# Rebuilding an expert router's chain, and gathering tokens by pairs of experts from one fp32 copy

## The chip, the core and the metric

The kernel runs on one core of one Trainium2 chip. The metric is the device time of one run in microseconds (us). The kernel before was run three times: median 1444.87 us, 1441.94 to 1446.6.

## What is computed

Two blocks of a network are applied to 256 tokens of width D = 1024. The first block is a mixer (a gMLP and an RWKV-7 recurrence side by side) and a hierarchical mixture of experts; the second is two layers of attention and feed-forward. Each sublayer's input is normalised, then scaled and shifted by vectors that are themselves products of a conditioning vector c with a weight matrix (the modulation). The change lies in the end of the mixer and in the mixture of experts:

```python
x = x + gate1[:, None, :] * y
h = _modulate(_rmsnorm(x, norm2_g[l]), shift2, scale2)
...
group_prob = jax.nn.softmax((ht @ rg_w + rg_b).astype(f32), axis=-1)
g_p, g_idx = lax.top_k(group_prob, 1)
exp_logits = (ht @ re_w + re_b).astype(f32).reshape(N, N_GROUPS, EXPERTS_PER_GROUP)
sel = jnp.take_along_axis(exp_logits, g_idx[:, :, None], axis=1)[:, 0]
e_p, e_idx = lax.top_k(jax.nn.softmax(sel, axis=-1), TOP_K)
e_p = e_p / jnp.sum(e_p, axis=-1, keepdims=True)
weights = g_p * e_p
...
return (jax.nn.silu(xbk @ w_gate[e]) * (xbk @ w_up[e])) @ w_down[e]
```

So a token picks one of 4 groups, then two of that group's 8 experts; the two results are added with their weights. There are 32 experts with a hidden width of 512; the three weight matrices of each are 2.1 MB in fp32, and all of them are read.

## The kernel before, in words

Everything is fp32, and the 256 tokens lie on the partitions in two halves i of 128. TensorE (PE) multiplies, VectorE (DVE), ScalarE (ACT) and GpSimd (POOL) do the rest, SyncE (SP) issues the loads.

**Modulation** (L179 to L241) is a generator. One step loads 256 rows of a weight matrix (1.05 MB) and multiplies them with c in 16 small matmuls into a PSUM buffer; DVE adds it to a sum in SBUF. Four steps make one of the vectors. Steps are spread over the kernel: `fill(n)` takes the next n, `need(j)` takes as many as vector j wants (L246 to L253), and tables (FILL_A, L33, and others) say how many are taken at which place. Eight are taken at the end of the recurrence, in front of the output projection (FILL_A[3]).

**The end of the mixer.** `project_out(kt)` (L845 to L867) turns one of eight slices of the mixer's output, splits it and the weights in high and low fp32r halves, and adds three products to four PSUM buffers, two halves of the tokens by two halves of the columns. L928 to L942 run it for all eight and add the gated result to x, one buffer of 128x512 after the other.

**The router** (L946 to L1049). x is turned (L963 to L967), multiplied with the 36 columns of router weights (L971), and scaled by the inverse norm (L973, L978). Then comes a chain of small DVE instructions: the maximum of the groups, the selected group's 8 logits, first and second maximum among them (`first_max`, L984 to L995), a mask M of 32 experts and the weights Wt (L1026 to L1032), the number of the largest count (L1039 to L1045) and the position of each token within its expert (L1047). The scale and shift of the modulation are brought to the layout of the gathered tokens (GS, L1052 to L1071). The normalised x is then written in two fp32r halves, xh by ACT and xl by a subtraction on POOL (L1074 to L1081), with the width in another order, because a weight row block takes every eighth column.

**Loads of expert weights** (L1084 to L1107). Each load is 1.05 MB, half a matrix. They go to 14 rotating slots (4 + 6 + 2 + MORE, where MORE is 2, L27). 18 loads are issued ahead of the first expert, in the order ORDER (L31); four of them go to buffers that have another use later (EARLY, L30), the twelfth to one of the two buffers of gathered tokens.

**The experts.** 64 slots are reserved for each expert; a pair j of experts fills 128 partitions. `gather(quad)` (L1187 to L1205) makes for two pairs a one-hot matrix D4 from the positions and, for each of eight slices of the width, four fp32r matmuls of 128x256 (two halves of tokens, high and low) into a PSUM buffer of their own; DVE and ACT in turn evict them with scale and shift to xg. `widen(j)` (L1207, matmuls L1216) multiplies with 4 loads of gate weights, and again with 4 of up weights; `gated` and `turned` (L1222, L1230) make the activation and turn it; `places(j)` (L1234 to L1249) turns the one-hot matrix back; `narrow(j)` (L1251, matmuls L1261) multiplies with 4 loads of down weights; `scatter(j)` (L1274, matmuls L1280 and L1282) adds the weighted result to the tokens. The loop (L1292 to L1320) takes pairs 0 to 9 and then 10 to 15. PE's order in it is the written one (`manual_schedule`): gate of pair j, turning of j-1, scatter of j-2, places of j-1, up of j, the gather for the next two pairs where j is odd, down of j-1. The other engines' order is a list scheduler's. After pair 9 a branch (`crowded`, L1119) looks whether any expert has more than 64 tokens; with these inputs none has, and the branch is not taken.

**Two lines elsewhere.** Behind the experts, `flip` (L358 to L412) turns and evicts a PSUM buffer twice, by ACT (L367) and by DVE (L379), which both read the same buffer.

## Time and profile before

| | |
|---|---|
| median of three runs | 1444.87 us (1441.94 to 1446.6) |
| the profiled execution | 1445.49 us |
| its span in the profile | 1443.7 us |
| PE busy (weight loads beside it: 1002.3 us) | 1356.1 us, 94% |
| DVE busy | 763.9 us, 53% |
| ACT busy | 576.5 us, 40% |
| POOL busy | 77.9 us |
| DMA | 400.42 MB, 277 GB/s in the mean |
| PE's granted clock, mean | 0.977 of full speed |

The profile is of one execution; times within it count from the start of its span. A busy engine is one with an instruction in work; a share over the whole span is a mean of stages with different limits, so the table alone doesn't tell what bounds a stage. The granted clock is 0.5 (1.2 GHz) or 1.0 (2.4 GHz) at a moment, and a mean over a stretch.

### The profile page before, as it was taken

To read this page: it belongs to the slowest core of one execution; us is meant where nothing else is said; L and a number is where in the kernel's file an instruction comes from. 1 tells how busy PE (TensorE), PEld (TensorE's weight loads), DVE (VectorE), ACT (ScalarE), POOL (GpSimd) and SP (SyncE) were. 2 spreads that over 40 slices of the span, in tenths; PEclk is the share of its full clock that TensorE was granted. 3 is DMA by queue.
4 is the path that set the end of the run, shared out by engine and by line. 5 is a ranking of instruction groups with operands and counts; after the bars stand their busy time and mean duration, and the time that the engine had idled before them with its cause. 6 is when DMAs were issued, how large, how long until landed. Compare 5 with 4: busy or idle time off the path is not lost.

```text
span 1443.7 us, 22926 instructions
## 1 busy us (share of the span) xinstructions
PE 1356.1 (94%) x9330; PEld 1002.3 (69%) x9330; DVE 763.9 (53%) x1507; ACT 576.5 (40%) x1020; POOL 77.9 (5%) x79
## 2 busy tenths in 40 slices
PE   6999999699999988989979989999998999999997
PEld 5888878444444434534348867899996897799997
DVE  5648767511221111111165885888876575766565
ACT  3543013411111111101166755554456685654544
POOL 1002000100000000000020230000021001100000
PEclk9989999799999999999989999999999999999999
DMA  9826479599999999999967564988775534555540
GB/s 361 295 69 251 164 274 380 226 365 426 426 427 426 427 427 402 391 426 427 427 246 252 196 228 146 336 276 311 286 248 181 172 117 149 184 196 196 178 150 30
DMA packets 138688, 400.42 MB, mean 277 GB/s; under 512 B 6562, under 2 KB 84658, under 8 KB 114003
## 3 DMA queue, kind: packets, MB, share of 16 engines
q1 hardware_dynamic: 138578, 398.91, 72.0%
q8 instruction: 75, 1.23, 0.3%
q14 instruction: 35, 0.28, 0.1%
HBM read 397.82 MB, written 1.05 MB: 276 GB/s over the span
## 4 chain that ended last, share of the span: by engine, by line
PE 44%; DMA 9%; DVE 3%; ACT 3%; issue 1%; POOL 0%; POOLq 0%; DVEq 0%; SPq 0%; ACTq 0%
PE pmm L416 8%; PE pmm L417 8%; PE pmm L418 8%; PE pacc L416 5%; PE pacc L417 5%; PE pacc L418 5%; DMA wruns<-in_moe_w_gate_dram 4%; DMA wruns<-in_moe_w_down_dram 3%; DMA wruns<-in_moe_w_up_dram 2%; PE pmm L190 1%; PE pmm L1261 1%; ACT sqj L294 1%; PE pmm L366 1%; PE pmm L1622 1%; PE pmm L435 1%
## 5 line engine op out<-in xcount | busy, mean ns | idle before, releaser
L416 PE MATMUL pmm<-hh,whi 128*128 128x256 f32 (+1 forms) x1040 | 296.4, 285 | 2.0 <-ACT whi L167 2.0
L418 PE MATMUL pmm<-hh,wlo 128*128 128x256 f32 (+1 forms) x1040 | 297.1, 286 | 0.2 <-DVE wlo L168 0.2
L417 PE MATMUL pmm<-hl,whi 128*128 128x256 f32 (+1 forms) x1040 | 295.5, 284 | 0.0
L1216 PE MATMUL pmm<-wruns,xg 128*64 128x512 f32 x1024 | 233.1, 595 | 7.1 <-DMA wruns<-in_moe_w_gate_dram 7.1
L168 DVE TENSOR_TENSOR wlo<-wcols,whi 128x1024 fp32r<-128x1024 f32 (+1 forms) x130 | 168.4, 1300 | 99.3 <-ACT whi L167 98.8
L416 PEld LDWEIGHTS pmm<-hh,whi 128*128 128x128 f32 (+1 forms) x1040 | 197.6, 190 | 8.6 <-issue 3.6
L417 PEld LDWEIGHTS pmm<-hl,whi 128*128 128x128 f32 (+1 forms) x1040 | 196.6, 189 | 1.4
L418 PEld LDWEIGHTS pmm<-hh,wlo 128*128 128x128 f32 (+1 forms) x1040 | 197.0, 189 | 0.6 <-DVE wlo L168 0.4
L167 ACT ACTIVATE whi<-wcols 128x1024 fp32r<-128x1024 f32 (+1 forms) x130 | 136.1, 1053 | 119.0 <-PE pmm L417 91.7
L1216 PEld LDWEIGHTS pmm<-wruns,xg 128*64 128x64 f32 x1024 | 81.8, 137 | 141.1 <-issue 115.8
L168 DVE TENSOR_TENSOR wlo<-wrows,whi 128x1024 fp32r<-128x1024 f32 x87 | 108.1, 1248 | 56.3 <-ACT whi L167 55.9
L167 ACT ACTIVATE whi<-wrows 128x1024 fp32r<-128x1024 f32 x87 | 91.7, 1061 | 90.5 <-PE pmm L417 45.5
L1261 PE MATMUL pmm<-wruns,em 128*64 128x512 f32 x512 | 118.4, 595 | 7.2 <-DMA wruns<-in_moe_w_down_dram 5.7
L1261 PEld LDWEIGHTS pmm<-wruns,em 128*64 128x64 f32 x512 | 38.5, 137 | 79.3 <-issue 62.4
L1270 ACT ACTIVATE o<-ay 128x512 fp32r<-128x512 f32 x32 | 20.2, 631 | 177.5 <-DVE ay L1269 177.5
L1269 DVE SCALAR_TENSOR_TENSOR ay<-pmm,wsl,ga 128x512 f32<-128x512 f32 x32 | 24.0, 751 | 105.8 <-PE pmm L1261 103.8
L1307 DVE TENSOR_TENSOR ay<-ay,pmm 128x512 f32<-128x512 f32 x16 | 11.0, 688 | 120.0 <-PE pmm L1216 120.0
L1248 DVE COPY wsl<-pmm 64x1 f32<-64x1 f32 x32 | 5.0, 156 | 130.7 <-PE pmm L1245 130.4
L417 PE MATMUL pacc<-wlo,ah 128*128 128x512 f32 x176 | 69.2, 393 | 0.0
L416 PE MATMUL pacc<-whi,ah 128*128 128x512 f32 x176 | 68.9, 391 | 0.0
L418 PE MATMUL pacc<-whi,al 128*128 128x512 f32 x176 | 68.6, 393 | 0.0
L1222 ACT ACTIVATE ay<-pmm 128x512 f32<-128x512 f32 x16 | 9.6, 598 | 109.4 <-PE pmm L1216 109.4
(533 smaller groups left out, 2217.3 us busy)
## 6 DMA issues: line engine op xcount, KB each, us to landing
wruns<-in_moe_w_gate_dram SPq DMA_DIRECT2D x64, 1024.0 KB, 19.5
wruns<-in_moe_w_up_dram SPq DMA_DIRECT2D x64, 1024.0 KB, 19.5
wruns<-in_moe_w_down_dram SPq DMA_DIRECT2D x64, 1024.0 KB, 19.6
wrows<-in_w_mod_dram SPq DMA_DIRECT2D x48, 1024.0 KB, 7.0
wcols<-in_w_ffn_gate_dram SPq DMA_DIRECT2D x22, 1024.0 KB, 5.2
wcols<-in_w_ffn_up_dram SPq DMA_DIRECT2D x22, 1024.0 KB, 6.3
wrows<-in_w_ffn_down_dram SPq DMA_DIRECT2D x22, 1024.0 KB, 5.2
wrows<-in_ada_w_dram SPq DMA_DIRECT2D x16, 1024.0 KB, 7.7
```

Source lines behind the costliest of these rows:

```text
L167: ACT.activation(hi, src, AF.Copy)
L168: (POOL if ahead else DVE).tensor_tensor(lo, src, hi.bitcast(F32), op=OP.subtract)
L190: PE.matmul(p[32 * g:32 * g + 32, 0:n].rearrange("p (a j) -> p a j", j=32), lhsT, groups(rhs)[:, g], start=first, stop=last, skip_group_ch ...
L294: ACT.activation(j, src, AF.Square, accum_out=ss)
L366: PE.matmul(p, src[:, i, 128 * kt:128 * kt + 128], dg[i], start=True, stop=True)
L416: PE.matmul(p, a[0], b[0], start=first, stop=False, skip_group_check=True)
L417: PE.matmul(p, a[0], b[1], start=False, stop=False, skip_group_check=True)
L418: PE.matmul(p, a[1], b[0], start=False, stop=last, skip_group_check=True)
L1216: PE.matmul(p[64 * a:64 * a + 64, :], xg[:, kt, lc(2 * j + a)], wt[a][:, k, :], start=kt == 0, stop=kt == KT - 1, skip_group_check=True)
L1261: PE.matmul(pd[n][64 * a:64 * a + 64, :], hT[:, f, 64 * a:64 * a + 64], wt[a][:, b, 512 * n:512 * n + 512], start=f == 0, stop=f == 3, ski ...
L1269: DVE.scalar_tensor_tensor(yf, pd[n], wsl, ga2[:, ns], op0=OP.mult, op1=OP.mult)
L1270: ACT.activation(oh[:, ns], yf, AF.Copy)
```

## The change

It edits five things.

- **The end of the mixer.** `project_out` is split: turning and splitting stay in it, the products move to `project_on(kt, i, w)`. The last two slices are done for tokens 0 to 127 first, then for tokens 128 to 255, and the gated sum of the first half runs while the second half's products do. The preparation of the router's weights (G2, rw, rb) is moved ahead of slice 4. The sums of squares of x are started per half.
- **The router.** PE, DVE and ACT get a written order. The transposes go by token half and four slices into one PSUM buffer. Maxima are taken over all 8 rows (two token halves by four groups) of 8 experts at once, and the chosen group is applied to the mask at the end. The mask and the counting matmuls are fp32r. The weights Wt are computed after the first one-hot matrix; the largest count (`most_`) moves into the loop, behind the gather of pair 1. Temporaries lie in one buffer `scr`.
- **Modulation.** Three of the eight steps in front of the output projection (FILL_A[3] 8 to 5) are taken behind the logits, and `need(5, 6, 7)` stands behind the issue of the weight loads. From there on `hold` is set and is not reset: the products of steps 1 to 3 of a vector are added up in one PSUM buffer, step 3 ends with an extra `yield`, and DVE adds the buffer in the step after it.
- **The gather.** xh and xl give way to one fp32 copy xr, written by ACT alone; POOL's subtraction goes. `gather(j)` works for one pair: eight slices of two fp32 matmuls of 128x128, four slices to a PSUM buffer, each slice evicted behind its own matmuls by DVE and ACT in turn. The gathered tokens go to a half of `xx`, which before that holds the transposed x. In the loop the gather of pair j+1 follows the up matmuls of pair j, for every j within a group.
- **Loads.** MORE is 4 instead of 2 (16 rotating slots), three buffers instead of four are used early, and 19 loads are issued ahead.

The function `crowded` is adapted to the new names. The core of the diff:

```diff
 BIG = 6
-MORE = 2
+MORE = 4
 GROUPS = (range(0, 10), range(10, 16))
 
-EARLY = {4: "em", 3: "ay", 11: "oo", 12: "xg"}
-ORDER = (0, 1, 2, 5, 6, 7, 8, 9, 10, 3, 4, 11, 12, 13, 14, 15, 16, 17)
-
-FILL_A = (0, 0, 2, 8, 0, 2)
+EARLY = {4: "em", 3: "ay", 11: "oo"}
+ORDER = (0, 1, 2, 5, 6, 7, 8, 9, 10, 3, 4, 11, 12, 13, 14, 15, 16, 17, 18)
+
+FILL_A = (0, 0, 2, 5, 0, 2)
 FILL_P = (0, 4, 2)
 FILL_E = 3
...
+    hold = []
...
-                    p = gv[-1]()
+                    held = bool(hold) and q > 0
+                    if not held or q == 1:
+                        p = gv[-1]()
                     for kt in range(2 * q, 2 * q + 2):
-                        products(p, cb(kt), wt[:, kt % 2, :], kt == 2 * q, kt == 2 * q + 1)
-                    if q == 0:
+                        products(p, cb(kt), wt[:, kt % 2, :], kt == (2 if held else 2 * q), kt == (7 if held else 2 * q + 1))
+                    if held and q == 3:
+                        yield
+                    if held and q < 3:
+                        pass
+                    elif q == 0:
                         ACT.activation(acc, p[:, 0:256], AF.Copy)
                     else:
                         DVE.tensor_tensor(acc, p[:, 0:256], acc, op=OP.add)
@@ -859,12 +866,14 @@
                 DVE.tensor_tensor(yl[:, kt, :], yf, yh[:, kt, :].bitcast(F32), op=OP.subtract)
             if kt % 2 == 0:
                 w_out.append(load_rows(A["w_out"][0], 128 * kt))
...
+            return split_w(w_out[-1][:, kt % 2:kt % 2 + 1, :])
+
+        def project_on(kt, i, hl):
+            hi, lo = hl
+            ts = slice(128 * i, 128 * i + 128)
+            for n in range(2):
+                ns = slice(512 * n, 512 * n + 512)
+                mm3(op[i][n], (yh[:, kt, ts], yl[:, kt, ts]), (hi[:, 0, ns], lo[:, 0, ns]), kt == 0, kt == 7)
...
+
+        G2, S2 = G1, modc[:, 3, :]
         DVE.scalar_tensor_tensor(G2, modc[:, 4, :], 1.0, colr("n2g", 8), op0=OP.add, op1=OP.mult)
...
+        for kt in range(4, 6):
+            w = project_out(kt)
             for i in range(2):
...
+                project_on(kt, i, w)
+
+        w = [project_out(kt) for kt in (6, 7)]
         for i in range(2):
...
+            for kt in (6, 7):
+                project_on(kt, i, w[kt - 6])
+        rr = [Rstd() for _ in range(2)]
+        halves = [slice(0, 512), slice(512, 1024)]
+        with tc.manual_schedule(engines=MAN):
+            for i in range(2):
+                for n, ns in enumerate(halves):
+                    xs = x_sb[:, i, ns]
+                    DVE.tensor_tensor(op[i][n], op[i][n], ga[:, n, :], op=OP.mult)
+                    DVE.tensor_tensor(xs, op[i][n], xs, op=OP.add)
+                    if i == 0:
+                        rr[0].square(n, xs)
+                if i == 0:
+                    rr[0].first()
+                    rr[0].second()
...
+        big = lambda n: pool.tile([128, D], F32, name=n, tag="big", bufs=1)
+        scr = big("scr")
...
+        xx = pool.tile([128, 2, KT, 128], F32, name="xx")
+        xr = pool.tile([128, 2, D], F32, name="xr")
...
+        def one_hot(D4, quad):
+            for i in range(2):
+                DVE.tensor_tensor(D4[:, i], pos[:, i, 4 * quad:4 * quad + 4, None].to_broadcast([128, 4, 64]),
+                                  slot[:, None, :].to_broadcast([128, 4, 64]), op=OP.is_equal)
+
+        with tc.manual_schedule(engines={_E.PE, _E.DVE, _E.Activation}):
+            pl = pacc()
...
+            turn_x(0, 0, True)
+            turn_x(0, 1, True)
+            rr[1].square(0, x_sb[:, 1, 0:512])
+            rr[1].square(1, x_sb[:, 1, 512:1024])
+            logits(0, 0)
+            turn_x(1, 0, False)
+            r = [rr[0].end()]
+            logits(0, 1)
+            rr[1].first()
+            rr[1].second()
+            turn_x(1, 1, False)
+            r.append(rr[1].end())
+            logits(1, 0)
+
+            for i in range(2):
+                ACT.activation(xr[:, i, :].rearrange("t (k p) -> t k p", k=KT),
+                               x_sb[:, i, :].rearrange("t (p k) -> t k p", k=KT), AF.Copy, scale=r[i])
+            logits(1, 1)
+
...
+            gor = pool.tile([128, 2, 128], F32R, name="gor")
+            gtr, onr = gor[:, 0, :], gor[:, 1, :]
+            DVE.tensor_copy(gtr, gt)
+            DVE.tensor_scalar(onr, gt, 0.0, 1.0, op0=OP.mult, op1=OP.add)
+            DVE.tensor_copy(GS, pg[:, 0:16])
+
+            hold.append(True)
+            fill(3)
...
+            DVE.tensor_reduce(m1, el, axis=AX.X, op=OP.max)
+            DVE.tensor_reduce(gm_, gl, axis=AX.X, op=OP.max)
+            DVE.tensor_tensor(c8, el, on8(m1), op=OP.is_equal)
+            DVE.tensor_tensor(gc, gl, on4(gm_), op=OP.is_equal)
+            DVE.scalar_tensor_tensor(c8, c8, -64.0, io, op0=OP.mult, op1=OP.add)
+            DVE.tensor_tensor(eg, gl, on4(gm_), op=OP.subtract)
...
+            DVE.tensor_tensor(c8, o1, o2, op=OP.add)
+            DVE.tensor_tensor(M.rearrange("p i (g e) -> p (i g) e", g=4), c8, on8(ogf), op=OP.mult)
+
+            p = pmm()
+            PE.matmul(p[:, 0:32], gtr, M[:, 0, :], start=True, stop=True, skip_group_check=True)
+            PE.matmul(p[:, 32:64], onr, M[:, 0, :], start=False, stop=False, skip_group_check=True)
+            PE.matmul(p[:, 32:64], gtr, M[:, 1, :], start=False, stop=True, skip_group_check=True)
+            DVE.scalar_tensor_tensor(pos, M.bitcast(F32), -1000.0, p[:, 0:64].rearrange("p (i e) -> p i e", i=2),
+                                     op0=OP.mult, op1=OP.add)
+            one_hot(D4, 0)
...
-        vI = pool.tile([128, 24], I32, name="vI")
...
-
-        xh = pool.tile([128, 2, D], F32R, name="xh")
-        xl = pool.tile([128, 2, D], F32R, name="xl")
-        for i in range(2):
-            xk = x_sb[:, i, :].rearrange("t (p k) -> t k p", k=KT)
-            ACT.activation(xh[:, i, :].rearrange("t (k p) -> t k p", k=KT), xk, AF.Copy, scale=r[i])
-            xf = big("xf")
-            ACT.activation(xf.rearrange("t (k p) -> t k p", k=KT), xk, AF.Copy, scale=r[i])
-            POOL.tensor_tensor(xl[:, i, :], xf, xh[:, i, :].bitcast(F32), op=OP.subtract)
...
+        def most_():
+
+            p = pmm()
+            for i in range(2):
+                PE.matmul(p[:, 0:32], ones, M[:, i, :].bitcast(F32), start=i == 0, stop=i == 1)
...
+        need(5, 6, 7)
...
-        def gather(quad):
-            D4 = pool.tile([128, 2, 4, 64], F32R, name="D4", bufs=2)
-            for i in range(2):
-                DVE.tensor_tensor(D4[:, i], pos[:, i, 4 * quad:4 * quad + 4, None].to_broadcast([128, 4, 64]),
-                                  slot[:, None, :].to_broadcast([128, 4, 64]), op=OP.is_equal)
-            xg = pool.tile([128, KT, 256], F32, name="xg", bufs=2)
-            for kt in range(KT):
+        def gather(j):
+
+            quad, pr_ = divmod(j, 2)
+            if pr_ == 0:
+                if quad:
+                    S_["quad", quad] = pool.tile([128, 2, 4, 64], F32, name="D4", bufs=2)
+                    one_hot(S_["quad", quad], quad)
+                else:
+                    S_["quad", quad] = D4
+            Dq = S_["quad", quad]
+            for g in range(2):
                 p = pmm()
-                n = 0
-                for i in range(2):
-                    for hx in (xh, xl):
-                        PE.matmul(p[:, 0:256], hx[:, i, 128 * kt:128 * kt + 128],
-                                  D4[:, i].rearrange("p e s -> p (e s)"), start=n == 0, stop=n == 3)
-                        n += 1
-                if kt % 2:
-                    ACT.activation(xg[:, kt, :], p[:, 0:256], AF.Identity, scale=G2r[:, kt:kt + 1], bias=S2r[:, kt:kt + 1])
-                else:
-                    DVE.tensor_scalar(xg[:, kt, :], p[:, 0:256], G2r[:, kt:kt + 1], S2r[:, kt:kt + 1], op0=OP.mult, op1=OP.add)
-            S_["quad", quad] = D4, xg
+                for k in range(4):
+                    kt = 4 * g + k
+                    ps = p[:, 128 * k:128 * k + 128]
+                    for i in range(2):
+                        PE.matmul(ps, xr[:, i, 128 * kt:128 * kt + 128],
+                                  Dq[:, i, 2 * pr_:2 * pr_ + 2, :].rearrange("p e s -> p (e s)"), start=k == 0 and i == 0,
+                                  stop=k == 3 and i == 1, skip_group_check=True)
+                    xg = xx[:, pr_, kt, :]
+                    if kt % 2:
+                        ACT.activation(xg, ps, AF.Identity, scale=G2r[:, kt:kt + 1], bias=S2r[:, kt:kt + 1])
+                    else:
+                        DVE.tensor_scalar(xg, ps, G2r[:, kt:kt + 1], S2r[:, kt:kt + 1], op0=OP.mult, op1=OP.add)
 
...
-                gather(g[0] // 2)
+                gather(g[0])
...
+                    if j is not None and j + 1 in g:
+                        gather(j + 1)
+                    if j == 0:
+                        most_()
                     if before is not None:
-                        if j is not None and j % 2 and j + 1 in g:
-                            gather((j + 1) // 2)
                         narrow(before)
```

## Rows read from the trace of the kernel before

**Rows 1.** Windows: stretch, length, busy PE PEld DVE ACT POOL, PEclk, DMA, GB/s

```profile
260.00:269.00 9.00, 0.12 (x2) 0.01 (x1) 8.17 (x30) 6.21 (x5) 4.70 (x2) 0.50 1.02 431
269.00:279.00 10.00, 9.11 (x48) 8.94 (x50) 5.04 (x20) 1.78 (x4) 0.00 (x0) 0.59 0.11 47
279.00:452.00 173.00, 173.00 (x870) 73.86 (x867) 32.01 (x61) 27.02 (x47) 0.00 (x0) 1.00 0.97 400
452.00:552.00 100.00, 89.83 (x418) 39.05 (x414) 17.33 (x33) 13.01 (x23) 0.00 (x0) 1.00 1.01 427
552.00:557.50 5.50, 0.00 (x0) 0.00 (x0) 0.07 (x1) 0.00 (x0) 0.00 (x0) 0.64 1.01 419
563.00:737.00 174.00, 163.75 (x772) 76.90 (x771) 30.13 (x55) 27.38 (x48) 4.33 (x2) 0.99 0.99 414
```

**Rows 2.** PE's waits, 279 to 737 us: total, count, longest

```profile
PE pmm L1216 <- DMA wruns<-in_moe_w_gate_dram: 7.1, 7, 1.3
PE pmm L1261 <- DMA wruns<-in_moe_w_down_dram: 5.7, 7, 1.2
```

**Rows 3.** Time line of PE at the branch, 557 to 563 us

```profile
557.60 0.55 PE L1198 MATMUL pmm<-D,xh 128*128 128x256 f32 x1 [5.95 <-PEq L1120]
...
562.83 21.02 PE L1216 MATMUL pmm<-wruns,xg 128*64 128x512 f32 x96
```

**Rows 4.** Time line of PE: one pair with a gather, and the last scatter

```profile
344.54 7.04 PE L1216 MATMUL pmm<-wruns,xg 128*64 128x512 f32 x32
...
354.51 7.09 PE L1216 MATMUL pmm<-wruns,xg 128*64 128x512 f32 x32
361.52 0.39 PE L1198 MATMUL pmm<-D,xh 128*128 128x256 f32 x1
...
365.55 7.09 PE L1261 MATMUL pmm<-wruns,em 128*64 128x512 f32 x32
...
736.67 0.63 PE L1282 MATMUL pacc<-o,DT 128*128 128x512 f32 x1
```

**Rows 5.** Time line of the router, 251 to 279 us, all engines

```profile
251.54 0.40 PE L418 MATMUL pacc<-whi,yl 128*128 128x512 f32 x1
...
253.59 1.28 DVE L942 TENSOR_TENSOR x_sb<-pacc,x_sb 128x512 f32<-128x512 f32 x2
...
260.16 0.42 DVE L978 SCALAR_TENSOR_TENSOR L<-pmm,rsr,rb 128x36 f32<-128x36 f32 x2 [2.08 <-PE pmm L971]
...
261.93 2.36 POOL L1081 TENSOR_TENSOR xl<-xf,xh 128x1024 fp32r<-128x1024 f32 x1 [42.01 <-ACT xf L1080]
...
262.57 1.75 DVE L989 TENSOR_TENSOR r_ac<-r_sl,r_am 128x16 f32<-128x16 f32 x1
...
269.01 0.17 DVE L1030 TENSOR_TENSOR M<-r_go,r_M 128x32 f32<-128x32 f32 x1
...
273.02 0.55 PE L1198 MATMUL pmm<-D,xh 128*128 128x256 f32 x1 [0.75 <-DVE D L1190]
...
278.81 13.95 PE L1216 MATMUL pmm<-wruns,xg 128*64 128x512 f32 x64
```

**Rows 6.** Time line of PE: one step of modulation

```profile
210.50 1.07 PE L190 MATMUL pacc<-wrows,csil 128*32 128x256 f32 x16
```

**Rows 7.** Time line of PE: fp32 matmuls of 128x128, 674 to 677 us

```profile
675.19 1.95 PE L435 MATMUL pmm<-ident,par 128*128 128x128 f32 x16
676.98 0.38 PE L1240 MATMUL pmm<-ident,D 128*128 128x128 f32 x2
```

**Rows 8.** Lines 367 and 379: ns shortest/median/longest; last, DVE's idle time

```profile
L367 ACT ACTIVATE hh<-pmm,modc,gc x32: 449/458/462, 741.9 to 1111.0; 128x128 fp32r<-128x128 f32 x32
...
L379 DVE TENSOR_SCALAR hf<-pmm,gc,modc x24: 399/405/411, 742.5 to 1111.2; 128x128 f32<-128x128 f32 x24
...
  ACT hh L367: 3.1, 7
```

**Rows 9.** SP's queue waits, 257 to 284 us: total, count, longest

```profile
SPq L149 <- PE pmm L1216: 25.6, 1, 25.6
```

More of the change, by code (lines that the diff above doesn't have):

```diff
@@ L968, in block @@
-        pl = pmm()
-        for i in range(2):
-            for kt in range(KT):
-                PE.matmul(pl[:, 64 * i:64 * i + 36], xT[:, kt, 128 * i:128 * i + 128], rw[:, kt, :],
-                          start=i == 0 and kt == 0, stop=kt == KT - 1, skip_group_check=True)
-        r = [rstd_x(i) for i in range(2)]
-        need(5)
-        need(6, 7)
-        L = pool.tile([128, 2, 36], F32, name="L")
-        for i in range(2):
-            DVE.scalar_tensor_tensor(L[:, i, :], pl[:, 64 * i:64 * i + 36], r[i], rb, op0=OP.mult, op1=OP.add)
@@ L997, in block @@
-        g4 = L[:, :, 0:4]
-        gm_, og = first_max(g4, 4, "g")
-        eg = t8("eg", 4)
-        DVE.tensor_tensor(eg, g4, bb(gm_, 4), op=OP.subtract)
-        ACT.activation(eg, eg, AF.Exp)
-        gs = t8("gs", 1)
-        DVE.tensor_reduce(gs, eg, axis=AX.X, op=OP.add)
-        pr = pool.tile([128, 2, 8, 4], F32, name="pr")
-        for i in range(2):
-            DVE.tensor_tensor(pr[:, i], L[:, i, 4:36].rearrange("p (g e) -> p e g", g=4),
-                              og[:, i, None, :].to_broadcast([128, 8, 4]), op=OP.mult)
@@ L1043, in block @@
-        DVE.tensor_reduce(most, pc[:, 0:32], axis=AX.X, op=OP.max)
-        mosti = pool.tile([128, 1], I32, name="mosti")
-        DVE.tensor_copy(mosti, most)
-        pos = pool.tile([128, 2, 32], F32, name="pos")
-        DVE.scalar_tensor_tensor(pos, M, -1000.0, p[:, 0:64].rearrange("p (i e) -> p i e", i=2), op0=OP.mult, op1=OP.add)
+        for kt in range(4, 6):
+            w = project_out(kt)
+            for i in range(2):
+                project_on(kt, i, w)
+        w = [project_out(kt) for kt in (6, 7)]
@@ L1172, in crowded @@
                             for b in range(2):
-                                PE.matmul(p, Dt[:, b, 128 * i:128 * i + 128], yo[:, b, ns], start=b == 0, stop=b == 1)
+                                PE.matmul(p, Dt[:, b, 128 * i:128 * i + 128], yo[b][n], start=b == 0, stop=b == 1)
                             DVE.tensor_tensor(to, p, ga2[:, ns], op=OP.mult)
                             DVE.tensor_tensor(x_sb[:, i, ns], x_sb[:, i, ns], to, op=OP.add)
+        most = pool.tile([128, 1], F32, name="most")
+        mosti = pool.tile([128, 1], I32, name="mosti")
+        def most_():
+            p = pmm()
+            for i in range(2):
+                PE.matmul(p[:, 0:32], ones, M[:, i, :].bitcast(F32), start=i == 0, stop=i == 1)
+            DVE.tensor_reduce(most, p[:, 0:32], axis=AX.X, op=OP.max)
+            DVE.tensor_copy(mosti, most)
+        need(5, 6, 7)
         em = pool.tile([128, 4, 512], F32, name="em")
@@ L1207, in widen @@
         def widen(j):
[L1209 removed]
+            xg = xx[:, j % 2]
             p = pmm()
@@ L1234, in places @@
         def places(j):
[L1235 to L1237 removed]
+            Dq, pr_ = S_["quad", j // 2], j % 2
+            Dp = [Dq[:, i, 2 * pr_:2 * pr_ + 2, :].rearrange("p e s -> p (e s)") for i in range(2)]
             p = pmm()
```

201 lines of the change are left out of this document (92 added, 109 removed).

## The prediction

> **What bounds the kernel now.** I read the windows table over the expert stage first, then PE's waits there, then the time line of one pair of experts, and last the time line of the router. [rows 1]: from 279 to 737 us the DMA moves 400 to 427 GB/s, which looks like a stage that waits for weights, but PE is busy for all of 279 to 452 and for nine tenths of the rest. [rows 2]: between 279 and 737 PE waited for the weights only 7.1 + 5.7 = 12.8 us; 5.95 us went at the branch behind the first ten pairs [rows 3]. So PE and DMA are almost level. A pair of experts is 12 loads of 1.05 MB, 29.5 us at 427 GB/s [rows 1]. On PE [rows 4] it is three groups of 32 instructions at 7.04 us and, from the first group's end to 354.51, 2.9 us for the turning, the scatter and the places: 24.1 us. Every second pair adds a gather of 4.03 us (361.52 to 365.55). PE's room is thus about 5 us of a pair, and what the stage has lost to the weights in all is 12.8 us. The router ahead of it is a chain on DVE [rows 5]: the last half of x ends at 254.87, the logits are there at 260.16, the expert mask at 269.18, PE's first gather starts at 273.02 and the first expert matmul at 278.81. PE does nothing from 260 to 269 and its granted clock falls to 0.5 [rows 1].
>
> **The router.** Today 30 DVE instructions take 8.17 us of the window from 260 to 269 [rows 1]; two of them run long beside POOL's subtraction for the low half of x (one is 1.75 us where its neighbours are 0.17 [rows 5]), together 3.7 us. That POOL work goes with the low half. The new order leaves 22 DVE instructions in front of the mask: 22 x 0.17 = 3.7 us, and I add 0.5 us for the one that stands behind ACT's exponential, since ACT first makes two copies of x. Finishing tokens 0 to 127 first puts the end of x at PE's last projection matmul (about 251.9) plus one multiply and one add of a half, 0.64 us each [rows 5]: 253.3 instead of 254.9. I take the logits at 257.8 (2.4 us earlier; DVE's fourteen small instructions for masks and columns now stand in front of them and fit while PE works), the mask at 262.0. Behind it stand three matmuls, the positions and the first one-hot tile, without the four weight and two maximum instructions that stand there today: 2.1 us instead of 3.8. The first gather starts at 264.1, 8.9 us earlier. The three modulation steps in the bubble cost PE 3 x 1.07 us [rows 6], hidden in the idle 9 us, and keep its clock up. They leave the place in front of the output projection, which waits on a chain of DVE and ACT there: I count nothing.
>
> **The gather.** It uses one fp32 copy where two fp32r halves stood, and it is made for a pair, 16 times where there were 8. No fp32 gather is in the trace; the nearest are fp32 matmuls of 128x128 by 128x128: eight of them are 16 instructions at 1.79/16 = 0.112 us (675.19 to 676.98 [rows 7]). A gather has 16 matmuls, so 32 instructions: 3.6 us, 3.8 with its start. Today a pair's share is 2.0 us. Already this adds 14 x 3.8 - 6 x 4.03 = 29 us inside the two groups of pairs, more than twice the 12.8 us that PE waits.
>
> The new gather also puts four slices of 128 columns in one PSUM buffer, and behind each slice stands its own eviction, by DVE and ACT in turn, before PE's next slice into the same buffer. Does PE's next slice wait for it? In [rows 8] DVE's L379 reads the buffer that ACT's L367 is just reading; neither writes it and neither needs the other's result, and yet DVE's idle time ahead of it, 3.1 us in 7 places, ends with L367. Users of one buffer on different engines are kept one behind the other. That a write of PE waits in the same way for a reader of other columns no row shows. I take it that it does, since the row nearest to it shows two mere readers in line. Then a slice is a round: four instructions, 3 x 0.112 + 0.275 = 0.61 us to their end, the eviction 0.405 us on DVE or 0.458 on ACT [rows 8], and two handovers of about 0.06: 1.16 us on average. Eight rounds are 9.3 us, less 0.7 us twice where PE needn't wait (the change of buffer, the last eviction), plus 0.2: **8.1 us** of PE's queue. The bounds are 3.8 us (no wait) and 8.6 (a weight load shown behind each wait).
>
> The Trainium skill, PSUM — Partial Sum Buffer, section "PSUM bank collisions raise a hardware error", goes further than the row: no two of PE, ACT and DVE may touch one bank in the same 32 partitions at once, other columns and mere reads included, so software has to order them. By that rule the sum is the one with 8.1 us, and by the row taken narrowly it is the one with 3.8; no run here shows PE's side of it.
>
> **The sum,** against the profiled execution, 1445.5 us (span 1443.7; 0.6 us over the median of the runs, 1444.9). From the first expert matmul, 278.81 [rows 5], to the end of the last scatter, 737.3 [rows 4], are 458.5 us. Out: 12.8 us of waits for weights (a pair will need 32.2 us on PE against 29.5 for its loads), 6 x 4.03 = 24.2 us of gathers, 5.2 us for the one behind the branch (557.60 to 562.83 [rows 3]). In: 14 x 8.1 = 113.4 us; behind the branch, at half the clock (PEclk 0.64 over 552 to 557.5, falling [rows 1]), rounds of 1.63 us: 11.5 us; 0.5 us for the maximum over experts, moved into the first pair. That is +83.2 us. The first expert matmul comes at 264.1 + 8.2 = 272.3, 6.5 us earlier. The stage ends 76.7 us later.
>
> **Loads.** The three modulation loads now stand behind the output projection's four on SP. The ring has six slots, so three expert loads (9, 10 and 12) need slots that are free only after the bubble, near 262, and what stands behind them in ORDER may wait too. Today all 18 are issued by 257 and SP then waits 25.6 us for the first slot [rows 9]. Load 3 would land near 272, just in time for the second half of the first group of matmuls; +0 to 3 us. With PE the bound this costs nothing later, and the two additional buffers gain nothing. **hold** is never cleared: later modulations off DVE take five steps instead of four, keep one PSUM buffer through three steps, and save DVE two additions each. In layer 0's attention four steps then fall due at one place: three loads and 3 x 1.07 us of PE [rows 6]. Between -1 and 3 x (1.07 + 2.46) = +11 us; I take +3, since the same steps leave the attention, where PE is busy. Sum: 1445.5 + 76.7 + 3 = **1525 us**; 1500 to 1550 with the bounds (rounds of 1.0 to 1.25 us, loads and hold as above).
>
> **Rivals.**
> - *PE doesn't wait for evictions of other columns.* For: no row shows such a wait. Against: [rows 8]. Then 14 x 3.8 us + 7 behind the branch, start 10.9 us earlier, hold as above: 83.2 - 113.4 - 11.5 + 53.2 + 7 - 10.9 + 3 = +10.6, 1456 us; 1446 to 1465. Slower all the same, since 3.6 us a gather is more than PE's room. Chance 0.13.
> - *Faster: the DMA stays the bound.* It idles today from about 270, when the 18 loads have landed, to 284.5 (47 GB/s in 269 to 279 [rows 1]). If the stage ended with its loads, the first slot 10.9 us earlier and one more load ahead (2.46 us) would give 1445.5 - 13 = 1432 us. It decides where a gather costs under about 2.5 us of PE, (24.2 + 5.2 + 12.8 - 7)/14; [rows 7] give 3.6 without any wait. Chance 0.06.
> - *The clock falls in the gathers.* In rounds PE streams for 0.45 us of 1.16. [rows 1] show 0.5 after idle stretches of 5 us and longer, and 1.00 from 452 to 552, where single waits of a microsecond stand between dense work. If it fell each time, a gather would be 11.5 us and the down matmuls behind it about 1.3 us longer: 14 x 4.7 = +66, 1591 us; in half of the pairs 1558. Chance 0.13.
> - *The change does not do what it says:* PE's order in the loop over the pairs is written out, and so are the three engines' in the router; I give that no chance of its own.
>
> **How the numbers follow.** Forecast 0.68, its own range 1500 to 1550. The range reaches down to the first rival and up to the clock falling in about half of the pairs: 1450 to 1565. That holds nearly all of the forecast, most of the first rival and half of the last. 0.3%, about what a measurement of this kernel can tell from no change, is 4.3 us. Faster is the second rival, 0.06; the first one is within 4.3 us only at its lower end: same 0.05; slower 0.89.
>
> **What the changed profile would show.** Right: PE's waits in the expert stage name ACT and DVE writing xx, some 100 of them of about 0.5 us, waits for weights near none, a DMA rate of about 390 GB/s, a pair at 32 us, first gather near 264. Wrong: gathers of 3.8 us in one piece, or waits for weights as long as now. A PEclk under 1 from 452 on would be the third rival.

## The result, and the profile after

The changed kernel takes **1558.8 us** (median of 4 runs, 1553.2 to 1561.3) against 1445.4 of the kernel before beside it: 1.078 times as long, 95% interval 1.075 to 1.082. The forecast was 1525, its own range 1500 to 1550, the whole range 1450 to 1565. So the sign and the stage were right, but the time lies above the forecast's own range, inside the whole one: the loss was 113 us where 80 were forecast. The profiled execution has a span of 1558.0 us, 114.3 over that of before. (Of the 13 executions of one experiment below, e8, two were slow, 1565.7 and 2356.2 us at a mean clock of 0.93 and 0.63; its time leaves them out, and since its trace is of one of the two, it gives no marks.)

Where the 114 us came from, by three marks in each trace (us):

| | first gather | first expert matmul | end of last scatter | between the two | behind it, to the end |
|---|---|---|---|---|---|
| before | 273.0 | 278.8 | 737.3 | 458.5 | 706.4 |
| forecast | 264.1 | 272.3 | 814.0 | 541.7 | 709.4 |
| after | 271.6 | 284.2 | 845.3 | 561.1 | 712.7 |

**The stage of the experts.** PE's waits between 284 and 830 us of the changed kernel (total, count, longest), where [rows 2] had two lines of waits for weights:

```profile
PE pmm L1260 <- DVE xx L1267: 33.7, 60, 0.9
PE pmm L1260 <- ACT xx L1265: 16.9, 30, 0.6
PE pmm L1260 <- PEq L1169: 5.6, 1, 5.6
...
PE pmm L1322 <- ACT em L1294: 0.7, 1, 0.7
```

No wait for weights is left. In their place stand 90 waits of the gather's matmuls (L1260) for the two engines that evict its slices (L1267, L1265). The time line of PE shows one gather and the down matmuls behind it; [rows 4] is the same stretch of before:

```profile
358.83 0.71 PE L1260 MATMUL pmm<-D,xr 128*128 128x128 f32 x4
360.11 0.71 PE L1260 MATMUL pmm<-D,xr 128*128 128x128 f32 x4 [0.56 <-DVE xx L1267]
361.42 0.71 PE L1260 MATMUL pmm<-D,xr 128*128 128x128 f32 x4 [0.60 <-ACT xx L1265]
362.71 1.16 PE L1260 MATMUL pmm<-D,xr 128*128 128x128 f32 x8 [0.58 <-DVE xx L1267]
364.37 0.71 PE L1260 MATMUL pmm<-D,xr 128*128 128x128 f32 x4 [0.50 <-DVE xx L1267]
365.68 0.71 PE L1260 MATMUL pmm<-D,xr 128*128 128x128 f32 x4 [0.60 <-ACT xx L1265]
366.97 1.22 PE L1260 MATMUL pmm<-D,xr 128*128 128x128 f32 x4 [0.58 <-DVE xx L1267]
368.12 8.20 PE L1322 MATMUL pmm<-wruns,em 128*64 128x512 f32 x32
376.15 7.03 PE L1278 MATMUL pmm<-wruns,xx 128*64 128x512 f32 x32
```

Four instructions, a wait of 0.5 to 0.6 us, four more: a round every 1.28 to 1.31 us. Behind the eviction of the first slice (359.65 to 360.05) PE's weight load and matmul start together:

```profile
359.65 0.40 DVE L1267 TENSOR_SCALAR xx<-pmm,GS 128x128 f32<-128x128 f32 x1
360.11 0.52 PEld L1260 LDWEIGHTS pmm<-D,xr 128*128 128x128 f32 x4 [0.76 <-DVE xx L1267]
```

Only at 362.71 do eight stand together, where the second PSUM buffer begins and nothing has to be waited for. From 358.83 to 368.12 are 9.3 us where a pair's share was 2.0. In the last round the four instructions take 1.22 us and no longer 0.71, and the 32 down matmuls behind it 8.0 us (368.12 to 376.15) and not 7.0: the clock has fallen. The windows of two such gathers, an early one and this one, of the down matmuls behind this one, and of the stretches at either clock (columns as in [rows 1]):

```profile
326.00:335.00 9.00, 5.58 (x36) 4.18 (x36) 2.24 (x5) 1.37 (x3) 0.00 (x0) 1.00 0.94 395
358.80:368.20 9.40, 5.98 (x36) 4.59 (x36) 2.24 (x5) 1.37 (x3) 0.00 (x0) 0.93 1.01 425
368.00:376.20 8.20, 8.20 (x35) 2.65 (x36) 0.69 (x1) 0.46 (x1) 0.00 (x0) 0.85 0.49 177
367.00:370.30 3.30, 3.30 (x10) 1.67 (x12) 0.00 (x0) 0.46 (x1) 0.00 (x0) 0.50 0.84 353
370.50:376.10 5.60, 5.60 (x28) 1.83 (x26) 0.59 (x1) 0.00 (x0) 0.00 (x0) 1.00 0.39 120
```

Summed from start to start over the stage, the gathers take 141.2 us where they took 29.4, widening and narrowing 351.7 where they took 360.7, everything else, with the idle time at the branch, 68.2 where it took 68.4.

**The router.** Its time line, all engines; the rows answer to [rows 5]:

```profile
254.42 13.18 SPq L149 DMA_DIRECT2D wruns<-in_moe_w_gate_dram  x3
...
254.86 0.16 DVE L336 SCALAR_TENSOR_TENSOR rsh<-ss,rshb 128x1 f32<-128x1 f32 x1 [0.73 <-ACT sqj L301]
...
254.94 0.69 DVE L971 TENSOR_TENSOR pacc<-pacc,ga 128x512 f32<-128x512 f32 x1
...
257.00 0.69 DVE L972 TENSOR_TENSOR x_sb<-pacc,x_sb 128x512 f32<-128x512 f32 x1
...
263.57 4.96 PE L191 MATMUL pmm<-wrows,csil 128*32 128x256 f32 x48
...
263.76 0.66 DVE L1075 SCALAR_TENSOR_TENSOR scr<-pacc,rsr,rb 128x32 f32<-128x32 f32 x4
...
268.60 0.42 DVE L239 TENSOR_TENSOR ga<-pmm,ga 128x256 f32<-128x256 f32 x1 [1.90 <-PE pmm L191]
...
269.90 0.23 DVE L1112 TENSOR_TENSOR M<-scr 128x64 fp32r<-128x64 f32 x1
...
271.62 1.19 PE L1260 MATMUL pmm<-D,xr 128*128 128x128 f32 x4 [0.86 <-DVE D L1006]
```

From the end of x (257.69) to the first gather are 13.9 us where it took 18.2 (254.87 to 273.02). So the new chain is 4.2 us shorter, and still the first expert matmul comes 5.4 us later: x itself is done 2.8 us later, and the first gather takes 12.6 us in place of 5.8, both at half the clock for all or most of it. Within the chain DVE stands still for 1.9 us at L239: that is the addition of the modulation from the bubble, which the scheduler has put between DVE's instructions for the mask and which waits for PE's 48 matmuls.

**Behind the experts** the kernel loses 6.3 us, at one place above all. PE's waits behind 829 us:

```profile
PE pmm L191 <- DVE gm L224: 10.1, 1, 10.1
```

Between the two layers PE stands for 10.1 us in front of a modulation's matmuls, whose products DVE has not finished. In the kernel before two waits of 1.4 and 3.7 us stand at this place.

### The profile page after: what moved, and what is told of

It is laid out like the page before. It is cut to its first block, busy times and chain, and to the rows that moved or that the text cites. A ratio compares the mean times of both kernels' runs of the same rounds, so it can differ in the third digit from the quotient of the medians.

```text
span 1558.0 us, 23535 instructions
## 1 busy us (share of the span) xinstructions
PE 1429.9 (92%) x9583; PEld 1039.2 (67%) x9583; DVE 765.2 (49%) x1526; ACT 583.0 (37%) x1052; POOL 73.4 (5%) x77
## 3 DMA queue, kind: packets, MB, share of 16 engines
q8 instruction: 78, 1.28, 0.3%
## 4 chain that ended last, share of the span: by engine, by line
PE 52%; DVE 4%; ACT 2%; issue 1%; DMA 0%; POOL 0%; DVEq 0%; ACTq 0%
PE pmm L423 7%; PE pmm L424 7%; PE pmm L425 7%; PE pmm L1278 6%; PE pacc L423 4%; PE pacc L424 4%; PE pacc L425 4%; PE pmm L1322 3%; PE pmm L1260 2%; PE pmm L191 1%; DVE xx L1267 1%; PE pmm L442 1%; PE pmm L373 0%; DVE wlo L168 0%; PE pmm L1685 0%
## 5 line engine op out<-in xcount | busy, mean ns | idle before, releaser
L1278 PE MATMUL pmm<-wruns,xx 128*64 128x512 f32 x1024 | 230.1, 604 | 0.0
L1278 PEld LDWEIGHTS pmm<-wruns,xx 128*64 128x64 f32 x1024 | 72.3, 139 | 140.7 <-issue 139.7
L1260 PE MATMUL pmm<-D,xr 128*128 128x128 f32 x512 | 101.2, 333 | 60.3 <-DVE xx L1267 35.8
L1260 PEld LDWEIGHTS pmm<-D,xr 128*128 128x128 f32 x512 | 77.3, 221 | 91.2 <-DVE xx L1267 49.1
L1322 PE MATMUL pmm<-wruns,em 128*64 128x512 f32 x512 | 123.1, 637 | 1.4 <-ACT em L1294 1.4
L1265 ACT ACTIVATE xx<-pmm,GS 128x128 f32<-128x128 f32 x64 | 29.3, 457 | 232.7 <-PE pmm L1260 232.7
L1267 DVE TENSOR_SCALAR xx<-pmm,GS 128x128 f32<-128x128 f32 x64 | 26.2, 409 | 99.0 <-PE pmm L1260 99.0
```

The lines of the kernel that those rows point to most:

```text
L1260: PE.matmul(ps, xr[:, i, 128 * kt:128 * kt + 128], Dq[:, i, 2 * pr_:2 * pr_ + 2, :].rearrange("p e s -> p (e s)"), start=k == 0 and i == 0 ...
L1265: ACT.activation(xg, ps, AF.Identity, scale=G2r[:, kt:kt + 1], bias=S2r[:, kt:kt + 1])
L1267: DVE.tensor_scalar(xg, ps, G2r[:, kt:kt + 1], S2r[:, kt:kt + 1], op0=OP.mult, op1=OP.add)
L1278: PE.matmul(p[64 * a:64 * a + 64, :], xg[:, kt, 64 * a:64 * a + 64], wt[a][:, k, :], start=kt == 0, stop=kt == KT - 1, skip_group_check=True)
L1322: PE.matmul(pd[n][64 * a:64 * a + 64, :], hT[:, f, 64 * a:64 * a + 64], wt[a][:, b, 512 * n:512 * n + 512], start=f == 0, stop=f == 3, ski ...
```

## The experiments

Ten kernels, each timed beside the kernel before (1444.4 to 1447.2 in these comparisons). The same marks for each profiled execution:

| | time | ratio, 95% interval | x to first gather | first expert matmul | stage | behind |
|---|---|---|---|---|---|---|
| before | | | 23.1 | 278.8 | 458.5 | 706.4 |
| after | 1558.8 | 1.075 to 1.082 | 20.4 | 284.2 | 561.1 | 712.7 |
| e1 evictions behind | 1457.0 | 1.005 to 1.010 | 17.7 | 270.5 | 464.5 | 713.0 |
| e2 own buffers | 1462.8 | 1.008 to 1.014 | 20.4 | 279.1 | 469.8 | 712.6 |
| e3 hold reset | 1553.7 | 1.071 to 1.076 | 20.4 | 287.0 | 557.2 | 707.9 |
| e4 no bubble | 1548.6 | 1.068 to 1.073 | 17.8 | 280.3 | 560.5 | 709.0 |
| e5 before, two a buffer | 1456.1 | 1.007 to 1.011 | 23.1 | 278.2 | 467.1 | 707.6 |
| e6 four experts, fp32 | 1441.6 | 0.9974 to 0.9994 | 18.6 | 278.0 | 456.5 | 707.0 |
| e7 filler | 1556.5 | 1.076 to 1.079 | 20.4 | 283.5 | 559.1 | 713.9 |
| e8 two repairs | 1446.3 | 1.0007 to 1.0025 | | | | |
| e9 fp32r halves | 1439.2 | 0.9956 to 0.9980 | 19.5 | 271.7 | 457.8 | 706.7 |
| e10 norm behind | 1439.4 | 0.9946 to 0.9973 | 18.6 | 273.4 | 457.8 | 707.6 |

"x to first gather" runs from DVE's first multiplication for x (L971, in the kernel before L941), since what lies ahead of it differs by up to 6.5 us between profiled executions of kernels that are alike up to there (247.5 to 254.0). e1's profiled execution, 1449.8 us, was 7 us under its median; the others, e8's apart, lie within 3 us of theirs.

**e1: evictions behind the four slices.**

```diff
                     for i in range(2):
                         PE.matmul(ps, xr[:, i, 128 * kt:128 * kt + 128], ...)
+                for k in range(4):
+                    kt = 4 * g + k
+                    ps = p[:, 128 * k:128 * k + 128]
                     xg = xx[:, pr_, kt, :]
                     if kt % 2:
                         ACT.activation(xg, ps, ...)
```

> The changed kernel with one edit: in the gather the evictions of a PSUM buffer's four slices stand behind all of its matmuls. Theory A (PE's next slice waits for the eviction of the slice before it in the same buffer, and the clock falls in these gaps): PE does 32 instructions in one piece, 3.6 to 4 us a gather where the changed kernel takes 9.2; the clock stays at full speed at the gather's end, so the down matmuls behind it take 7.1 us for 32 again and not 8.1. 12 gathers of 9.2 become 3.8, two that the trace shows at 12.7 become 7, and 12 times 1 us of slow clock goes: 1558.8 - 65 - 11 - 12 = 1471 us, some us more if loads become late again, since a pair on PE is then 28 us against 29.5 for its loads: 1465 to 1485. Rival B (the cost is the fp32 matmuls and their weight loads themselves, the waits only show it): a gather stays at 7 us or more and the time over 1530.

**e2: a buffer for each slice.**

```diff
             for g in range(2):
-                p = pmm()
                 for k in range(4):
                     kt = 4 * g + k
-                    ps = p[:, 128 * k:128 * k + 128]
+                    ps = pmm()[:, 0:128]
```

> The changed kernel with one edit: each of the eight slices of a gather has a PSUM buffer of its own (of the four that rotate), as in the kernel before; the eviction stands behind its slice as in the changed kernel. Theory A: the wait comes from sharing a buffer, so PE runs on into the next buffer: 3.6 to 4.5 us a gather (the fifth slice needs the first buffer back, which was evicted long before), time 1465 to 1485 us as with the evictions behind. Rival B (PE waits for each eviction however the buffers lie, or the matmuls themselves cost this): a gather of 7 us or more and over 1530 us.

Both make the gather short, by two quite different edits with the same matmuls and evictions. PE's time line in e1:

```profile
360.88 3.84 PE L1260 MATMUL pmm<-D,xr 128*128 128x128 f32 x32
364.65 7.09 PE L1325 MATMUL pmm<-wruns,em 128*64 128x512 f32 x32
```

3.77 us for the 32 instructions, in e2 also 3.77, and the down matmuls are back at full speed. Theory A holds and rival B falls. Both times came out just under the 1465 to 1485 expected: a pair takes 27.7 us on PE, under its loads' 29.5, and still PE's waits name no weights in either. That the loads which are ahead at the start last to the end is the likely reason; no run tests it. (In e2 PE stood for another 4.5 us behind the branch, in the middle of the gather, without a cause that the profile names; that is most of its 5.3 us over e1's stage, and it stays open.)

**e5: the suspected cause alone, in the kernel before.** Its fp32r gather, with two slices to a PSUM buffer:

```diff
             for kt in range(KT):
-                p = pmm()
+                if kt % 2 == 0:
+                    p2 = pmm()
+                p = p2[:, 256 * (kt % 2):256 * (kt % 2) + 256]
```

> The kernel before with the suspected cause alone: in its gather of four experts two slices of 256 columns share a PSUM buffer, the eviction of the first standing between them; fp32r halves, loads and router as before. Theory: each of the four second slices waits for the eviction in front of it (543 ns on DVE in the kernel before), some 0.8 us each with drain and handovers: a gather 7.2 to 7.6 us instead of 4.03, six times 3.3 and twice 4 to 5 us, in all 28 us, of which the 12.8 us of waits for weights can take up a part: 15 to 28 us over the kernel before. Rival (the wait belongs to the new fp32 form of the gather, not to a shared buffer): no change, within 3 us.

Each second slice waits, 32 times, and 11.6 us are lost by the medians (interval of the ratio: 10.7 to 15.5). PE's waits from 265 us on:

```profile
PE pmm L1200 <- DVE xg L1207: 20.7, 32, 0.7
...
PE pmm L1264 <- DMA wruns<-in_moe_w_down_dram: 0.9, 1, 0.9
```

A gather takes 7.64 us, at the upper end of what was expected, the seven of the stage cost 27.6 us more, and the first one, ahead of it, 5.3. The kernel's loss is at the lower end of the 15 to 28 expected or just under it, since 18.2 us of late weights went at the same time: widening and narrowing take 342.5 us, where the kernel before needs 360.7. That is more than the 12.8 us that [rows 2] name, and it shows what that view leaves out. A matmul of L1216 is recorded for 592 ns, while the next one follows after 220; so up to 0.37 us of each wait lies under the record before it, and shorter ones don't show at all. On the weight-load side of PE in the kernel before, 19 waits end with a load's landing where rows 2 count 14:

```profile
PEld pmm L1216 <- DMA wruns<-in_moe_w_gate_dram: 15.4, 11, 2.2
PEld pmm L1261 <- DMA wruns<-in_moe_w_down_dram: 12.8, 8, 2.1
```

The Trainium skill, Perfetto Trace Analysis, section "Identifying the Most-Contended Engine", says of busy time, not of waits, that the pipelined matmuls' is not a good measure of how close a kernel is to its limit, and names the weight loads' in its place; the counts of waits here, 19 against 14, point the same way.

**e7: PE kept busy while it waits.**

```diff
+            pf = pmm()
             for g in range(2):
...
+                    if kt < 7:
+                        PE.matmul(pf, xr[:, 0, 0:128], xr[:, 0, 0:512], start=True, stop=True)
```

> The changed kernel with work added: behind each slice of the gather but the last PE does one more fp32 matmul of 128x512 (0.44 us) into a PSUM buffer that nobody reads, so that it is busy while it waits for the eviction. Theory (the clock falls at the gather's end because PE stands idle in its gaps): the down matmuls behind a gather take 7.1 us for 32 again, not 8.1, and gathers stay at 8.7 to 9.0 us: 10 to 18 us less, 1540 to 1549, although PE has 7 us more work in each pair's gather. Rival (the clock falls for another reason, or the fill lies in line and not beside the wait): the same or slower, 1556 to 1600.

The windows from 285 to 600 us, e7 first and then the changed kernel:

```profile
285.00:600.00 315.00, 315.00 (x1508) 142.50 (x1506) 48.71 (x104) 42.37 (x83) 0.00 (x0) 1.00 0.89 365
```

```profile
285.00:600.00 315.00, 285.00 (x1368) 128.73 (x1366) 48.69 (x104) 43.07 (x83) 0.00 (x0) 0.96 0.88 359
```

The clock stays at full speed and the down matmuls behind a gather take 6.9 us from start to start (367.98 to 374.89 in the time line of e7) and not 8.0. That settles the clock's cause: it fell because PE waited. But the time is 2 us less, no difference that can be told, in the rival's band: the fill itself makes a gather 9.8 us. The gathers of the stage take 7.9 us more than in the changed kernel, and widening and narrowing 11.3 less. A pair takes 33.7 us in place of 34.15.

**e3 and e4: the modulation.** e3 puts `hold.clear()` behind `need(5, 6, 7)`; e4 has

```diff
-FILL_A = (0, 0, 2, 5, 0, 2)
+FILL_A = (0, 0, 2, 8, 0, 2)
...
-            hold.append(True)
-            fill(3)
```

> The changed kernel with one edit: hold is reset behind the three steps in the bubble, so that later modulations take four steps again. Theory: the 6.3 us that the changed kernel takes longer behind the last scatter (712.7 against 706.4 us) come from the fifth step, which moves all later steps by one or more places: 1552.5 us, the stretch behind the last scatter 706 to 708 us. Rival (the loads' order or the clock after the experts makes it): no change, 1557 to 1561 us.

> The changed kernel with the modulation put back: eight steps in front of the output projection, none in the bubble, no hold. Theory: the tail is that of the kernel before (706 us behind the last scatter, -6), and the addition of the modulation no longer stands in DVE's chain of the router, where it waited 1.9 us for PE and took 1 us: the first gather starts 2 to 3 us after the logits' chain earlier, against which the three steps lie in front of the output projection again (3.2 us on PE, hidden or not). First gather at 268.5 to 272.5 (271.6 now), time 1547 to 1556. Rival (the steps in the bubble are free, as the change means them, and before the projection they cost their 3.2 us): first gather at 274 or later.

e3 does what was expected: 5 us less, 707.9 us behind the last scatter, and the wait of 10.1 us is gone; in its place stand those of the kernel before. In e4 the time lies in the expected range (the first gather at 267.7, 0.8 us ahead of its own), and the stretch from x to the first gather falls by 2.6 us, to 17.8; DVE now goes from the logits to the mask without a gap, 261.97 to 265.86. e1 has 17.7 with the bubble, the other four profiled executions with it 20.4: in e1's PE's clock stayed up longer, 0.87 over 254 to 260 against 0.50 in the changed kernel's six microseconds ahead of 263.75, so the logits came earlier. DVE waits for the bubble there too:

```profile
262.14 0.42 DVE L239 TENSOR_TENSOR ga<-pmm,ga 128x256 f32<-128x256 f32 x1 [1.42 <-PE pmm L191]
```

From the copy of GS to the mask DVE takes 6.5 us in the changed kernel, 6.0 in e1 and 4.0 in e4.

The three steps in front of the output projection cost nothing there: from the first step to the projection's first matmul PE takes 29.6 us with eight steps (before, e4) and with five (after; 30.4 to 30.7 in e1, e2, e3 and e7). So the bubble was no free place: it costs 2.0 to 2.6 us in DVE's chain and, by hold, 5 us later.

**e8: e1 and e4 together.**

> The changed kernel with the two repairs that leave its gather by pairs: evictions behind the four slices (e1) and modulation back in front of the projection (e4). Theory: the repairs add up. e1's stage of 464.5 us, e4's first gather at 267.7 with 5.4 us for it, and the tail of the kernel before, 706: 267.7 + 5.4 + 464.5 + 706 = 1443.6 and 2 us around the span, 1440 to 1448, level with the kernel before. Rival (e1's early start of 265.2 was the bubble's doing): 1450 or more.

They add up as expected, to the kernel before's time within 0.3%: e1 alone gives back 101.8 us of the medians, e4 alone 10.2, both together 112.5.

**e6: four experts at once from the fp32 copy.** `gather` is called as in the kernel before, and without the bubble (e4); its core:

```diff
+            for kt in range(KT):
+                ps = pmm()[:, 0:256]
+                for i in range(2):
+                    PE.matmul(ps, xr[:, i, 128 * kt:128 * kt + 128], Dq[:, i].rearrange("p e s -> p (e s)"), ...)
+                xg, ps = xx[:, :, kt, :], ps.rearrange("p (a c) -> p a c", a=2)
```

> The changed kernel, its router, single fp32 copy and loads, but the gather made for four experts at once in a PSUM buffer per slice (two matmuls of 128x256, one eviction), and the modulation put back in front of the output projection as in e4_no_bubble. Theory: a gather is 32 instructions in 4.0 us, eight times instead of sixteen, and PE needs 26 us a pair against 29.5 for the loads, so the stage waits for weights again (10 us or more in all) and ends with them: first expert matmul 4 to 6 us after where e4 has its first gather, 272 to 275; stage 450 to 458 us; tail 706: 1430 to 1441 us, 3 to 15 under the kernel before. Rival (the router gains nothing that the loads don't take back, or fp32 at 256 columns costs twice fp32r): 1444 to 1460.

The gather did not come to 4.0 us. PE's time line:

```profile
364.18 7.17 PE L1253 MATMUL pmm<-D,xr 128*128 128x256 f32 x32
371.28 7.09 PE L1314 MATMUL pmm<-wruns,em 128*64 128x512 f32 x32
```

7.1 us for 32 instructions, 0.222 us each, where the fp32r ones at the same 256 columns took 4.03/32 = 0.126 [rows 4]. fp32 costs 1.8 times as much here as the two fp32r halves that it replaced; the rival, which said twice, was right in that. The time is between the two expectations, 1441.6, just under the kernel before, because PE's longer gathers fill the room in which it used to wait for weights: no wait for weights is left, and the stage is 456.5 us with gathers that cost 22 us more.

**e9: the new router with the old gather.** xh and xl are back, but xl by DVE:

```diff
+            def low(i):
+                DVE.scalar_tensor_tensor(xl[:, i, :]..., x_sb[:, i, :]..., r[i], xh[:, i, :].bitcast(F32)...,
+                                         op0=OP.mult, op1=OP.subtract)
```

one ahead of the chain, one behind the mask, MORE = 3, no bubble. **e10** moves `rr[0].first()` and `rr[0].second()` behind the four multiplications and additions of x.

> The changed kernel's router, token halves and written order with the gather of the kernel before: two fp32r halves (the low one by one DVE instruction per token half, the first while PE makes the logits, the second while it makes the positions, none on POOL), four experts at once, a PSUM buffer per slice; modulation in front of the projection as in e4_no_bubble; 15 rotating slots, 18 loads ahead. Theory: what costs in e6 is that fp32 at 256 columns takes PE twice as long (7.1 us a gather); the gather is 4.03 us again, PE no longer bounds the stage and waits for weights 10 to 25 us. First gather within 1 us of e6's (268.6), first expert matmul at 274 to 275.5; the stage 448 to 457 us, held by the loads; tail 706: 1430 to 1439 us, 5 to 14 under the kernel before. Rival (the loads end when they end: their first slot comes free when the first expert matmuls do, and the rest is theirs): stage 458 as before, 1440 us, level with e6.

> e9 with one edit: the three small instructions on the first token half's sum of squares stand behind the four multiplications and additions of x instead of between the halves, where DVE waited 0.9 us for ACT. Theory: the second half of x is ready 1.6 us earlier (0.93 of wait and the instructions beside it), the first gather 0.5 to 1.6 us earlier, since the first half's norm comes later but is needed only behind its logits; the time 0 to 2 us under e9's, hardly to be told from it, the trace decides. Rival (the norm of the first half becomes the late one: ACT's copies wait for it): the first gather at the same place or later.

e9 takes 1439.2 us, 0.2 to 0.4% under the kernel before. Its gathers take 3.97 us, and PE waits for weights again:

```profile
PE pmm L1285 <- DMA wruns<-in_moe_w_gate_dram: 6.7, 7, 1.3
...
PE pmm L1329 <- DMA wruns<-in_moe_w_down_dram: 5.5, 6, 1.2
```

The stage is 457.8 us, as long as before: here the rival holds, the loads end when they end. What is left is the earlier start, 271.7 where it was 278.8 (3.3 us of it is x, which came earlier in this execution, and 3.6 the way from x to the first gather). e10 has its 1.0 us between x and the first gather, and no difference in time that can be told.

## Why the prediction was right, and where it was not

The forecast's reason held, and it was tested from both sides: taken out of the changed kernel it gives back 102 us (e1), put alone into the kernel before it costs 11.6 (e5). PE's write to a PSUM buffer waits for the eviction of other columns of it. No row of before had shown PE's side; after shows it 90 times in the stage. That is also what the Trainium skill, PSUM — Partial Sum Buffer, section "PSUM bank collisions raise a hardware error", asks software to do, other columns included; the order was kept here with a semaphore wait at six of a gather's eight slices, 90 in 15 gathers; the other two slices start a buffer.

The first rival (no such wait, 1456) and the second (loads stay the bound) fell. The third, *the clock falls in the gathers*, was put as an alternative and is true beside the forecast, in part: the clock falls, in most gathers only in the last round and at the start of the down matmuls behind it. That its price for half of the pairs, 1558, is the measured time is chance. Of the signs, the waits came as said (90, some 100 forecast, and none for weights), but a pair took 34.15 us and not 32, the DMA moved 359 GB/s from 285 to 600 us and not 390, and the first gather started at 271.6 and not 264.

Term by term, 34.6 us were missing between the forecast's 79.7 and the 114.3 of the two spans; the terms below make 35, and what is left is under 1 us:

- **A gather in the groups, 8.1 us: 128.5/14 = 9.2 measured, +15 us.** A round was put at 1.16 us, 1.0 to 1.25 with its bounds, and is 1.28 to 1.31. The step that failed is the term for a slice's four instructions, put at 0.61 us: the value named as the upper bound, 8.6, "a weight load shown behind each wait", is nearer to what happens (0.71 us), and at full clock a gather is 8.7 to 8.8 us. The handovers, put at 0.06 us each from no row, take 0.05 to 0.06 behind an eviction and 0.09 to 0.11 in front of one. The rest, mostly 0.4 to 0.5 us a gather, is the clock in the last round; one gather of the second group, at half the clock from its fourth round on, took 11.2.
- **Waits for weights, -12.8 us: -9.0.** Two errors against each other. Late weights cost the kernel before 23 us (360.7 less the 337.6 us that e1 needs for widening and narrowing), not the 12.8 that the view of waits names; and the clock took back 14 (351.7 less 337.6). With the 6 to 7 us that it costs the 14 gathers (128.5 less 8.7 each), the fallen clock is worth some 20 of the 34.6 us, more than the mis-sized round: the rival's mechanism, which the forecast left out of its sum.
- **The gather behind the branch, 11.5 us: 12.7.**
- **The first expert matmul, -6.5 us: +5.4.** The first gather was put at 8.2 us, at full clock, which the matmuls in the bubble were to keep up; the clock is low there as it was before [rows 1], 0.72 over the 8 us ahead of the gather and 0.5 in it, and the gather took 12.6 (+4.4). The first gather's start, 264.1, was 7.5 us too early: x was done 3.9 us behind PE's last projection and not 1.4, since all four of DVE's instructions for the second half, 2.75 us, came behind PE's end, where two of 0.64 were counted, and between the halves DVE lost 0.9 us, mostly in a wait for ACT's sum of squares (e10 takes that out); PE's logits ran at half the clock; the projection itself ended 1.8 us later; and DVE's chain held the modulation's addition, which e4 and e1 price at 2.0 to 2.6 us. That the bubble would be free on DVE's side was not asked at all: the step named PE's cost (3 x 1.07, hidden) and forgot who waits for PE's result.
- **hold, +3 us: +6.3,** within its bounds of -1 to 11, and for the reason given, a step that comes later than its place; the place was the change of layers, not layer 0's attention.
- **Loads** behave as said: SP stands from 254.4 to 267.6 in front of loads whose slots the modulation holds, and it costs nothing, as no wait for weights follows. The 3.6 us for an fp32 gather without waits was right (3.77 in e1 and e2).

## What to carry to other kernels

Slices that share a PSUM buffer are cheap only if nobody reads the buffer before PE has written all of them: put the evictions behind the last slice, or give each slice its own buffer. A bubble on one engine is a free place only if nobody in the chain beside it waits for what is put there; ask who is handed the result, in which engine's order the receiver stands, and at which clock the filling engine runs. And where matmuls are recorded longer than their spacing, count waits from start to start or on the weight-load side, not from the idle time between records.

## What was not expected of the hardware

Waits of only 0.5 to 0.6 us, one in each 1.28 us, were enough to lower PE's clock: in seven of the nine gathers that the first group makes in its loop the last round ran at the 1.2 GHz level, the rounds ahead of it at 2.4, and the first 2 us or so of the dense down matmuls behind it at 1.2 too. With work in the waits the granted clock stayed at 1.00 (e7). It stayed there also in e5, where waits of 0.6 to 0.7 us stand between pieces of eight instructions and not of four:

```profile
285.00:550.00 265.00, 252.17 (x1242) 107.92 (x1240) 45.78 (x88) 36.85 (x66) 0.00 (x0) 1.00 0.99 411
```

And an fp32 matmul instruction with 256 columns took 0.222 us where fp32r took 0.126, so that one fp32 copy saves memory and the making of the low half, but costs PE time: 7.1 us a gather where the two halves take 4.
